# Second and third place change in seven products: the order of weight sums in a down projection

## The chip, the cores and the metric

The kernel runs on one core of one Trainium2 chip. The metric is the device time of one execution in microseconds (us). The engines of the core are named as in the profile: PE multiplies matrices, DVE (VectorE) and ACT (ScalarE) work element by element, POOL (GpSimd) does a few small operations and issues some transfers, and SP issues most of the transfers. The transfers themselves run on 16 DMA engines.

## What is computed

Two layers, each of three residual blocks with a layer norm behind it. The change lies in the first and the third block of each layer, the feed-forward ones, so it is passed four times in an execution.

```python
def swiglu_ffn(x, w_gu, w_down):
    a, u = jnp.split(x @ w_gu, 2, axis=-1)
    return (jax.nn.silu(a) * u) @ w_down
...
for l in range(DEPTH):
    x = layer_norm(DEEPNORM_ALPHA * x + 0.5 * swiglu_ffn(x, ffn1_w_gu[l], ffn1_w_down[l]), ln1_g[l], ln1_b[l])
    x = layer_norm(DEEPNORM_ALPHA * x + hybrid_mixer(...), ln2_g[l], ln2_b[l])
    x = layer_norm(DEEPNORM_ALPHA * x + 0.5 * swiglu_ffn(x, ffn2_w_gu[l], ffn2_w_down[l]), ln3_g[l], ln3_b[l])
```

Here x has 512 tokens of 1024 features, and the inner width DFF is 2816, that is 22 chunks of 128. Everything is in float32.

## The kernel before

**Numbers in two parts.** Every operand of a matmul is split in a rounded part and a rest (`split`, L158): ACT writes the rounded part (L159, tiles with an h at the end: `uh` for weights, `hh` for inner activations), and DVE then writes the rest (L160, tiles with an l: `ul`, `hl`). `mm3` (L165) makes three matmuls of such a pair: rounded by rounded (L168), and the two mixed ones (L169, L170 in the trace).

**Weights in units.** Weights come as a list of items that is taken in a fixed order. A unit is 128 x 1024 numbers and lies in one of six buffers (`UBUFS`). `Weights.pump` (L50) makes the next unit, that is its split and, where needed, the load of its raw weights, as soon as one of the six is given back by `W.done`; raw weights lie in two buffers of 1 MB (`raw`). `W.get` hands out units in the order of the list. So the place at which a split is asked for is set by the place in the list and by the `W.done` that frees a buffer.

**The gate stage** (`glu7`, L517) makes the inner activations `hT` two chunks at a time, in seven products of its own with `xh`, `xl`, `Th`, `Tl`. In its last pass (fp = 10) it ends with two groups on `Th`, `Tl`, an activation (L556) and a product on DVE (L563). Two kinds of its instructions matter below: the sums that DVE reads out of a bank before PE writes it again (L547), and L556 and L563, after which the memory pool of the gate stage is closed (L624) and the pool of the down stage, with `hh`, `hl` and `s1`, is opened in the same memory.

**The down stage** multiplies the first eight chunks of `hT` by the first 1024 rows of the down weights in seven products instead of eight (Strassen's scheme in Winograd's form). The activations are cut in A11, A12, A21, A22 (first figure: tokens 0 to 255 or 256 to 511; second: chunks 0 to 3 or 4 to 7), the weights in B11, B12, B21, B22 (rows, columns). Each product has two halves g = 0, 1 of two chunks, each half takes one unit, and one half is 12 matmuls of 512 columns. The order before:

| product | banks | activations | weights |
|---|---|---|---|
| 1 | low | A11 | B11 |
| 2 | left | A12 | B21 |
| 3 | high | `fifth`: A21 - A22 | B11 + B12 |
| 4 | low, on top | what `fifth` left in A11 | B11 + B12 + B22 |
| 5 | right | `third`: A12 plus that | B22 |
| 6 | low, on top | what `fifth` left in A21 | B12 + B22 |
| 7 | low, on top | A22 | B12 + B22 + B11 + B21 |

Between them, `into` (L710) adds finished banks into the residual `Y` with the instruction L714, two for each pair of banks; chunk 8 comes ahead of product 7, and chunks 9 to 21 behind it, as plain products.

**The sums of weights** are made by the DMA engines (`down_items`, L340). For each half g a tile `R[g]` has two columns. When the first unit of B11 is made, `begin` (L351) lets SP load B11 and B12 into them (L356), and lets POOL issue accumulating transfers (`add`, L348, its instruction L349) of 512 KB each: B12 onto column 0 of both halves, then B22 onto column 1 of both. `cut` (L363) makes a unit from a column (the splits `uh<-R` and `ul<-R`), and where it says so it then issues the next `add` onto the same column: B22 after the first cut of column 0, B21 after the second. The adds are kept in the order in which the program states them; `R` uses the two buffers (tag "S") in which the gate stage held its own weight sums.

**The operands** come from a generator, `operands` (L663), two halves ahead of their use: `ahead` (L696) starts with the two halves of A11, split early, and the first operand of the list, and each half of a product asks for one more before its matmuls (L724). `fifth` (L642) makes three subtractions on DVE (L647 into `s1`, L648 and L649 in place in A21 and A11) and then splits `s1`. `operand` splits a part of `hT` as it is. There are four pairs of `hh` and `hl`.

**Order.** After the very first pass `self.pin` is False: the splits aren't held to the order of the program. When the program is built, a scheduler lays out a fixed order for each engine from dependencies, the order of the program as priority and its own estimates of durations. On the chip each engine then takes its instructions in that order; one that waits holds up all behind it.

Of the kernel before, what the change touches and what calls it, by code (L numbers as in the profile page):

```python
# [24 lines left out]
ALPHA = (2 * DEPTH) ** 0.25  # L25
# [67 lines left out]
class Trunk:  # L93
# [246 lines left out]
    def down_items(self, w, key, R, row):  # L340

        def block(i, j, g):
            r0 = i * 512 + g * 256
            return w[r0 : r0 + 256, j * 512 : (j + 1) * 512].rearrange("(k p) c -> p k c", p=P)

        def add(g, x, i, j):  # L348
            self.tc.keep_in_program_order(self.nc.gpsimd.dma_start(R[g][:, x], block(i, j, g), accum_op=ALU.add))  # L349

        def begin(go):  # L351
            def f(v, hi, lo):
                for g in range(2):
                    R[g] = self.spool.tile([P, 2, 2, 512], F32, tag="S", name=self.nm("R"), bufs=2)
                    for x in range(2):
                        self.nc.sync.dma_start(R[g][:, x], block(0, x, g))  # L356
                    add(g, 0, 0, 1)
                for g in range(2):
                    add(g, 1, 1, 1)
                return go(v, hi, lo)  # L360
            return f

        def cut(g, x, *after):  # L363
            def go(v, hi, lo):
                hv, lv = (t.rearrange("p (k c) -> p k c", k=2) for t in (hi, lo))
                self.split(hv, lv, R[g][:, x])
                for a in after:
                    add(g, *a)
                return hv, lv
            return (None, None, None, go)  # L370

        p1, p2, p3 = (self.wide_item(w, j * 512, i, (key, "b", i, j)) for i, j in ((0, 0), (1, 0), (1, 1)))
        p1[0] = p1[0][:3] + (begin(p1[0][3]),)
        return (p1 + p2 + [cut(g, 0, (0, 1, 1)) for g in range(2)]
                + [cut(g, 0, (0, 1, 0)) for g in range(2)] + p3 + [cut(g, 1) for g in range(2)]
                + [row] + [cut(g, 0) for g in range(2)])

# [97 lines left out]
    def ffn(self, g_, b, out=None):  # L475
        nc, tc, W = self.nc, self.tc, self.W
        with ExitStack() as ctx:
# [150 lines left out]
            def pair():  # L628
                return [pool.tile([P, 512], F32R, tag=tag, name=self.nm(tag), bufs=TAIL) for tag in ("hh", "hl")]

            def part(g, i, j):

                return hT[:, j * 4 + 2 * g : j * 4 + 2 * g + 2, i * 256 : (i + 1) * 256]

            def operand(src):
                hh, hl = (v.rearrange("p (f t) -> p f t", f=2) for v in pair())
                self.split(hh, hl, src)
                return hh, hl
# [3 lines left out]
            def fifth(g):  # L642

                a11, a21, a22 = part(g, 0, 0), part(g, 1, 0), part(g, 1, 1)
                hh, hl = (v.rearrange("p (f t) -> p f t", f=2) for v in pair())
                s1 = self.s1[:, g]
                nc.vector.tensor_sub(s1, a21, a22)  # L647
                nc.vector.tensor_sub(a21, a11, a21)  # L648
                nc.vector.tensor_sub(a11, s1, a11)  # L649
                self.split(hh, hl, s1)  # L650
                return hh, hl

            def third(g):

                nc.vector.tensor_add(part(g, 0, 1), part(g, 0, 1), part(g, 0, 0))
                return operand(part(g, 0, 1))

            def whole(f):
                hh, hl = pair()
                self.split(hh, hl, hT[:, f, :])  # L660
                return hh, hl

            def operands():  # L663
                for g in range(2):
                    yield operand(part(g, 0, 1))
                for g in range(2):
                    yield fifth(g)
                for g in range(2):
                    yield operand(part(g, 0, 0))
                for g in range(2):  # L670
                    yield third(g)
                for g in range(2):
                    yield operand(part(g, 1, 0))
                yield whole(8)
                for g in range(2):
                    yield operand(part(g, 1, 1))
                for f in range(9, NF):
                    yield whole(f)

            def seventh(banks, u, h, new):  # L680

                for f in range(2):
                    for i, b_ in enumerate(banks):
                        ts = slice(i * P, (i + 1) * P)
                        self.mm3(b_, (h[0][:, f, ts], h[1][:, f, ts]), (u[0][:, f, :], u[1][:, f, :]),
                                 new and f == 0, False, skip_group_check=True)
                self.step()

            def down(f, u, h, t, q):
# [3 lines left out]
                         skip_group_check=True)  # L693

            split = operands()
            ahead = [(hv[0][:, g], hv[1][:, g]) for g in range(2)] + [next(split)]  # L696

            def chunk(f):
                u, h = W.get(), ahead.pop(0)
                ahead.append(next(split))  # L700
                for i, (t, q) in enumerate(((0, 0), (0, 1), (1, 0), (1, 1), (2, 1), (3, 1), (2, 0), (3, 0))):
                    down(f, u, h, t, q)
                    if i % 4 == 3:
                        self.step()
                W.done()

            low, high = [acc[t][0] for t in (2, 3)], [acc[t][1] for t in (2, 3)]
            left, right = [acc[t][0] for t in (0, 1)], [acc[t][1] for t in (0, 1)]

            def into(banks, t0, q, scale, sign=ALU.add):  # L710

                for i, b_ in enumerate(banks):
                    y = self.Y[:, t0 + i, q * 512 : (q + 1) * 512]
                    nc.vector.scalar_tensor_tensor(out=y, in0=y, scalar=scale, in1=b_, op0=ALU.mult, op1=sign)  # L714

            for n, (banks, new, more) in enumerate((
                    (low, True, (0, 0, ALPHA)), (left, True, None), (high, True, (0, 1, ALPHA)),
                    (low, False, (0, 1, 1.0, ALU.subtract)), (right, True, None),
                    (low, False, (2, 1, ALPHA, ALU.subtract)), (low, False, None))):
                if n == 6:  # L720
                    chunk(8)
                for g in range(2):
                    u, h = W.get(), ahead.pop(0)
                    ahead.append(next(split))  # L724
                    seventh(banks, u, h, new and g == 0)
                    W.done(2 if n == 0 and g == 1 else 1)
                if more:
                    into(banks, *more)
# [400 lines left out]
```

## Time and profile before

| what | value |
|---|---|
| runs before, median (lowest to highest of 3) | 1840.15 us (1836.89 to 1842.22) |
| the profiled execution, its own time | 1839.6 us |
| span of that execution in the profile | 1837.8 us |
| mean granted clock of PE | 0.991 |
| moved by DMA | 205.87 MB, 112 GB/s on the mean |
| accumulating adds, POOL | 32 of 512 KB, 8.1 us from issue to landing (median) |
| loads into `R`, SP | 16 of 512 KB, 5.2 us |
| first matmul of the four down stages | 233.58, 795.17, 1143.14, 1705.70 us from the span's start |

How to read it: the profile shows one execution. "Busy" is the time in which an engine had an instruction under way; matmuls overlap, so PE can be busy and yet not at its full pace. In a row of a timeline stand the start, the duration, the engine, the line, the operation, what it writes and reads, and in brackets how long the engine had been idle before and what ended that. In a table of waits stand the total, the number and the longest. The granted clock is the share of its full clock that PE was allowed. In the table of stretches (length, busy time and instructions of each engine, clock, share of the DMA engines' time, GB/s) the DMA share can come out a little over 1.

### The profile page before, as it was taken

The numbers are of one execution on the slowest core, as the hardware profiler recorded it, in microseconds if no ns is written. First come the engines' busy times: TensorE is split into PE (matmuls) and PEld (weight loads), VectorE is DVE, ScalarE is ACT, GpSimd is POOL, SyncE is SP. The second block draws the span as 40 slices with busy tenths as digits, with TensorE's granted clock in tenths as the row PEclk, the third lists the DMA queues.
The fourth block names the chain that finished last, engine by engine and source line by source line (L and its number), as shares of the span: only waits on it lengthen the run. The fifth ranks groups of instructions, "written<-read, shape, count | busy, mean of one in ns | idle before, by whom it ended". The sixth has DMA issues, their size and how long they took to land.

```text
span 1837.8 us, 29295 instructions
## 1 busy us (share of the span) xinstructions
PE 1801.7 (98%) x12074; PEld 1634.5 (89%) x12074; DVE 1341.4 (73%) x1942; ACT 880.5 (48%) x1439; POOL 123.8 (7%) x104
## 2 busy tenths in 40 slices
PE   9999989999999999989999999899999999999898
PEld 9999978887789999978899999788877899999786
DVE  7888785656758788876688887747567687887745
ACT  4455553278713455554235555432785234555530
POOL 0000010111110000020000001001111100000101
PEclk9999999999999999999999999999999999999999
DMA  5233475223122323484223236641233122334731
GB/s 183 93 127 103 148 196 161 64 81 91 49 91 69 116 93 101 140 195 161 92 65 97 93 101 196 163 155 47 81 93 92 46 93 93 112 118 137 185 114 46
DMA packets 151991, 205.87 MB, mean 112 GB/s; under 512 B 4657, under 2 KB 116017, under 8 KB 151857
## 3 DMA queue, kind: packets, MB, share of 16 engines
q1 hardware_dynamic: 143152, 187.23, 31.5%
q0 software_dynamic: 8704, 16.78, 5.3%
q8 instruction: 94, 1.54, 0.4%
q14 instruction: 41, 0.33, 0.1%
HBM read 201.89 MB, written 2.10 MB: 111 GB/s over the span
## 4 chain that ended last, share of the span: by engine, by line
PE 81%; DVE 5%; issue 5%; ACT 4%; DMA 3%; POOL 1%; SPq 0%; POOLq 0%; DVEq 0%; ACTq 0%
PE ps L170 26%; PE ps L168 26%; PE ps L169 26%; DMA R<-in_ffn_w_down_dram 2%; ACT sw L898 1%; PE ps L428 1%; DVE ul L160 1%; DMA raw<-in_ffn_w_gu_dram 1%; ACT uh L159 1%; ACT b L940 1%; ACT b L934 1%; DVE Y L464 1%; POOL sw L900 1%; DVE st L454 1%; DVE Y L461 0%
## 5 line engine op out<-in xcount | busy, mean ns | idle before, releaser
L168 PE MATMUL ps<-xh,uh 128*128 128x256 f32 (+1 forms) x1616 | 482.0, 298 | 0.2 <-ACT uh L159 0.2
L170 PE MATMUL ps<-xh,ul 128*128 128x256 f32 (+1 forms) x1616 | 479.1, 297 | 0.7 <-DVE ul L160 0.7
L169 PE MATMUL ps<-xl,uh 128*128 128x256 f32 (+1 forms) x1616 | 478.7, 296 | 0.4 <-DVE xl L160 0.2
L159 ACT CAST uh<-raw 128x1024 fp32r<-128x1024 f32 (+1 forms) x325 | 291.7, 914 | 220.2 <-PE ps L169 137.4
L160 DVE TENSOR_TENSOR ul<-raw,uh 128x1024 fp32r<-128x1024 f32 (+1 forms) x325 | 336.9, 1050 | 81.7 <-ACT uh L159 81.0
L168 PE MATMUL ps<-Th,uh 128*128 128x256 f32 x1152 | 319.1, 277 | 0.0
L169 PE MATMUL ps<-Tl,uh 128*128 128x256 f32 x1152 | 318.7, 277 | 0.0
L170 PE MATMUL ps<-Th,ul 128*128 128x256 f32 x1152 | 318.3, 276 | 0.0
L168 PEld LDWEIGHTS ps<-xh,uh 128*128 128x128 f32 x1616 | 307.9, 191 | 10.6 <-issue 1.6
L170 PEld LDWEIGHTS ps<-xh,ul 128*128 128x128 f32 x1616 | 307.9, 191 | 9.6 <-DVE ul L160 1.1
L169 PEld LDWEIGHTS ps<-xl,uh 128*128 128x128 f32 x1616 | 308.0, 191 | 8.5 <-DVE xl L160 0.8
L168 PE MATMUL ps<-uh,hh 128*128 128x512 f32 x640 | 256.2, 400 | 16.0 <-ACT hh L159 16.0
L170 PE MATMUL ps<-uh,hl 128*128 128x512 f32 x640 | 254.6, 398 | 4.8 <-DVE hl L160 4.8
L169 PE MATMUL ps<-ul,hh 128*128 128x512 f32 x640 | 252.4, 394 | 0.0
L159 ACT CAST uh<-S 128x1024 fp32r<-128x1024 f32 x144 | 151.1, 1049 | 153.0 <-PE ps L169 148.0
L160 DVE TENSOR_TENSOR ul<-S,uh 128x1024 fp32r<-128x1024 f32 x144 | 175.9, 1222 | 62.3 <-ACT uh L159 61.7
L168 PEld LDWEIGHTS ps<-Th,uh 128*128 128x128 f32 x1152 | 216.7, 188 | 0.0
L169 PEld LDWEIGHTS ps<-Tl,uh 128*128 128x128 f32 x1152 | 216.7, 188 | 0.0
L170 PEld LDWEIGHTS ps<-Th,ul 128*128 128x128 f32 x1152 | 216.3, 188 | 0.0
L168 PEld LDWEIGHTS ps<-uh,hh 128*128 128x128 f32 x640 | 122.7, 192 | 42.3 <-ACT hh L159 17.7
L170 PEld LDWEIGHTS ps<-uh,hl 128*128 128x128 f32 x640 | 122.2, 191 | 35.3 <-DVE hl L160 7.4
L169 PEld LDWEIGHTS ps<-ul,hh 128*128 128x128 f32 x640 | 122.4, 191 | 26.8
(141 smaller groups left out, 2249.2 us busy)
## 6 DMA issues: line engine op xcount, KB each, us to landing
raw<-in_ffn_w_gu_dram SPq DMA_DIRECT2D x86, 1024.0 KB, 5.6
raw<-in_ffn_w_down_dram SPq DMA_DIRECT2D x40, 1024.0 KB, 5.0
raw<-in_w_in_dram SPq DMA_DIRECT2D x18, 1024.0 KB, 5.3
R<-in_ffn_w_down_dram POOLq DMA_DIRECT2D x32, 512.0 KB, 8.1
R<-in_ffn_w_down_dram SPq DMA_DIRECT2D x16, 512.0 KB, 5.2
raw<-in_w_in_dram SPq DMA_DIRECT2D x8, 512.0 KB, 4.6
raw<-in_w_out_dram SPq DMA_DIRECT2D x8, 512.0 KB, 6.1
raw<-in_w_out_dram SPq DMA_DIRECT2D x4, 1024.0 KB, 4.9
```

Source lines behind the costliest of these rows:

```text
L159: a = self.nc.scalar.copy(hi, src)
L160: b = self.nc.vector.tensor_sub(lo, src, hi.bitcast(F32))
L168: mm(out, ah, bh, start=start, stop=False, **kw)
L169: mm(out, ah, bl, start=False, stop=False, **kw)
L170: mm(out, al, bh, start=False, stop=stop, **kw)
L428: nc.tensor.transpose(b[:, c * P : (c + 1) * P], src[:, c * P : (c + 1) * P], self.ident)
L454: nc.vector.bn_stats(out=st[:, h, :], in_=y[:, hs])
L464: nc.vector.scalar_tensor_tensor(out=y[:, hs], in0=y[:, hs], scalar=rs, in1=b[:, hs], op0=ALU.mult, op1=ALU.add)
L898: nc.scalar.copy(sw[q * 32 : q * 32 + 32, :n], src[o * 32 : o * 32 + 32, :n])
L900: nc.gpsimd.tensor_mul(sw[:, :n], sw[:, :n], S)
L934: nc.scalar.activation(s[kv][:, cc, :nk], s[kv][:, cc, :nk], AF.Exp, bias=m[:, cc : cc + 1], scale=SCALE, accum_out=den[:, cc : cc + 1])
L940: nc.scalar.activation(s[kv][:, cc, :nk], s[kv][:, cc, :nk], AF.Copy, scale=den[:, cc : cc + 1])
```

## The change

The third product of the table above becomes the second, and the second the third. In the list of weights the two units of B11 + B12 come ahead of those of B21; in `operands` `fifth` comes ahead of the split of A12; and the triple of banks, flag and `into` moves with them, so that the high banks are added into `Y` one product earlier. Nothing else is changed, and the number of instructions of every kind stays.

```diff
-        return (p1 + p2 + [cut(g, 0, (0, 1, 1)) for g in range(2)]
+        return (p1 + [cut(g, 0, (0, 1, 1)) for g in range(2)] + p2
                 + [cut(g, 0, (0, 1, 0)) for g in range(2)] + p3 + [cut(g, 1) for g in range(2)]
                 + [row] + [cut(g, 0) for g in range(2)])
...
             def operands():
                 for g in range(2):
+                    yield fifth(g)
+                for g in range(2):
                     yield operand(part(g, 0, 1))
-                for g in range(2):
-                    yield fifth(g)
                 for g in range(2):
                     yield operand(part(g, 0, 0))
...
-                    (low, True, (0, 0, ALPHA)), (left, True, None), (high, True, (0, 1, ALPHA)),
+                    (low, True, (0, 0, ALPHA)), (high, True, (0, 1, ALPHA)), (left, True, None),
                     (low, False, (0, 1, 1.0, ALU.subtract)), (right, True, None),
                     (low, False, (2, 1, ALPHA, ALU.subtract)), (low, False, None))):
```

## The prediction, made before the changed kernel ran

> **What bounds the kernel now.** The page comes first, then the list of waits, then the four places that the waits point at. TensorE (PE) is busy for nearly the whole span, so only what it waits for can be won or lost. The kernel has four down projections of seven products each, and among the waits of PE two rows belong to them alone (columns: total us, times, longest):
>
> ```profile
> PE 1801.7 (98%) x12074; PEld 1634.5 (89%) x12074; DVE 1341.4 (73%) x1942; ACT 880.5 (48%) x1439; POOL 123.8 (7%) x104
> ```
>
> ```profile
> PE ps L168 <- ACT hh L159: 16.0, 4, 4.3
> ```
>
> ```profile
> PE ps L170 <- DVE hl L160: 4.8, 4, 1.6
> ```
>
> So once per down projection PE waits for the rounded operand `hh`, and right after for its rest `hl`: 20.8 us together. The table of stretches prices it. Its first row is the second product of the first down projection, undisturbed; the other four are the third product of each (columns: length, PE busy, granted clock, DMA share, GB/s):
>
> ```profile
> 239.05:244.53 5.48, 4.97 (x17) 1.00 1.10 262
> 244.53:257.31 12.78, 6.45 (x16) 0.73 0.81 136
> 806.12:819.69 13.57, 6.87 (x16) 0.75 0.81 135
> 1154.10:1167.96 13.86, 6.87 (x16) 0.75 0.81 140
> 1716.66:1730.26 13.60, 6.38 (x16) 0.78 0.81 135
> ```
>
> The four third products take 53.8 us where 4 x 5.48 = 21.9 would do: **31.9 us** are lost, 8.0 per stage. 20.8 are waits; the other 11.1, 2.8 per stage, are matmuls at half clock after the wait. Two stretches around the first wait and one around a shorter wait elsewhere show when the clock falls (PE, PEld, DVE, ACT, POOL busy, clock):
>
> ```profile
> 246.34:249.75 3.41, 1.09 (x5) 0.56 (x3) 1.68 (x2) 1.28 (x2) 0.09 (x1) 1.00 0.68 124
> 249.75:256.58 6.83, 4.30 (x9) 2.98 (x10) 6.83 (x10) 5.90 (x8) 2.34 (x2) 0.50 0.76 116
> ```
>
> ```profile
> 453.00:456.41 3.41, 2.32 (x36) 2.09 (x32) 2.42 (x4) 3.34 (x7) 0.00 (x0) 1.00 0.33 91
> ```
>
> 3.41 us with PE 68% idle were followed by 6.83 us at half clock; 3.41 us with 32% idle were not.
>
> Why is the operand late? ACT's and VectorE's (DVE) rows in order of time, first stage:
>
> ```profile
> 228.12 1.05 ACT L159 CAST uh<-raw 128x1024 fp32r<-128x1024 f32 x1 [1.46 <-PE ps L169]
> 229.07 0.84 ACT L553 ACTIVATE Q<-Q 128x768 f32<-128x768 f32 x1
> 230.97 1.05 ACT L159 CAST uh<-raw 128x1024 fp32r<-128x1024 f32 x1 [1.06 <-PE ps L169]
> 232.42 0.38 ACT L556 ACTIVATE s<-ps 128x256 f32<-128x256 f32 x1 [0.39 <-PE ps L170]
> 233.66 1.05 ACT L159 CAST uh<-R 128x1024 fp32r<-128x1024 f32 x1 [0.86 <-PE ps L169]
> 234.62 1.14 ACT L159 CAST hh<-hT 128x512 fp32r<-128x512 f32 x2
> 235.66 0.62 ACT L159 CAST hh<-s 128x512 fp32r<-128x512 f32 x1
> 236.70 1.05 ACT L159 CAST uh<-R 128x1024 fp32r<-128x1024 f32 x1 [0.42 <-DMA R<-in_ffn_w_down_dram]
> 247.00 1.05 ACT L159 CAST uh<-R 128x1024 fp32r<-128x1024 f32 x1 [9.24 <-DMA R<-in_ffn_w_down_dram]
> 249.51 1.05 ACT L159 CAST uh<-R 128x1024 fp32r<-128x1024 f32 x1 [1.47 <-DMA R<-in_ffn_w_down_dram]
> 250.53 0.62 ACT L159 CAST hh<-s 128x512 fp32r<-128x512 f32 x1
> ```
>
> ```profile
> 230.35 0.42 DVE L547 TENSOR_TENSOR Q<-Q,ps 128x256 f32<-128x256 f32 x1
> ...
> 233.85 0.42 DVE L563 SCALAR_TENSOR_TENSOR hT<-ps,s 128x256 f32<-128x256 f32 x1 [0.36 <-PE ps L170]
> 234.31 0.69 DVE L647 TENSOR_TENSOR s<-hT 128x512 f32<-128x512 f32 x1
> 234.92 1.22 DVE L160 TENSOR_TENSOR ul<-R,uh 128x1024 fp32r<-128x1024 f32 x1
> 236.05 1.29 DVE L160 TENSOR_TENSOR hl<-hT,hh 128x512 fp32r<-128x512 f32 x2
> ...
> 248.07 1.23 DVE L160 TENSOR_TENSOR ul<-R,uh 128x1024 fp32r<-128x1024 f32 x1 [7.19 <-ACT uh L159]
> ```
>
> Call X0, X1 the sums B11+B12 of the two halves g, and Y0, Y1 the same with B22 added. 233.66 and 236.70 split X0 and X1; 247.00 and 249.51 split Y0 and Y1, which only the fourth product needs. 250.53 is the operand of the **third** product, half 1. It stands behind Y0 and Y1 in both queues and waits for two transfers that it does not use. PE stood idle for it, not for a weight.
>
> What holds the sums is POOL's queue and the DMA engines:
>
> ```profile
> 221.72 1.35 POOL L349 DMA_DIRECT2D R<-in_ffn_w_down_dram  x1 [220.41 <-DMA R<-in_ffn_w_down_dram]
> 227.15 2.44 POOL L349 DMA_DIRECT2D R<-in_ffn_w_down_dram  x2 [4.08 <-DMA R<-in_ffn_w_down_dram]
> 231.15 1.23 POOL L349 DMA_DIRECT2D R<-in_ffn_w_down_dram  x1 [1.55 <-DMA R<-in_ffn_w_down_dram]
> 236.88 1.21 POOL L349 DMA_DIRECT2D R<-in_ffn_w_down_dram  x1 [4.51 <-DVE hl L160]
> 241.12 1.20 POOL L349 DMA_DIRECT2D R<-in_ffn_w_down_dram  x1 [3.02 <-DVE Y L714]
> ```
>
> ```profile
> L349 POOL DMA_DIRECT2D R<-in_ffn_w_down_dram x1: 1707/1707/1707, 227.9 to 227.9; - x1
> DMA to landing us min/median/max: 13.0/13.0/13.0
> ```
>
> ```profile
> L349 POOL DMA_DIRECT2D R<-in_ffn_w_down_dram x1: 1207/1207/1207, 791.5 to 791.5; - x1
> DMA to landing us min/median/max: 5.9/5.9/5.9
> ```
>
> ```profile
> 243.00:246.50 3.50, 0.00 (x0) 1.00 1.13 206
> ```
>
> The six issues are, in order, X0, X1, the two sums in R's column 1, Y0, Y1. X1, issued at 227.15, is there for the split at 236.70, some 9.5 us later. The third lands at 227.9 + 13.0 = 240.9, and only 0.2 later Y1 is issued, although X1's split had ended by 239.1 (236.70 + 1.05 + 1.22, with a little between): I read this as at most three sums under way at once. With all DMA to themselves the sums move at 206 GB/s, so one of 0.524 MB takes 2.55 us. In the second stage X1 lands at 791.5 + 5.9 = 797.4.
>
> **The change part by part.** No instruction and no transfer is added or removed; four pairs change places.
>
> *Unit order.* X0's split comes to where B21's first split stands (228.12), X1's to 230.97, B21's to 233.66 and, the sixth buffer being free only after half a product, some 3 us on. These places follow from unit buffers: each row there was released by PE, not by data. But X1 is not there at 230.97. Will the built order still put it there? The order of now placed Y0 and Y1 ahead of work whose inputs were there some 8 us before them, so whoever laid it out took the sums for much faster than they are; I take it that X1's split stands at its early place, ahead of the activation L556. Bounds: no wait at all (X1 set behind L556), or the full one.
>
> *What the full wait costs, first stage.* ACT stands at X1 until 236.70, as now. DVE takes X1's rest at 237.78 (1.08 after the cast starts, as 248.07 after 247.00) for 1.13 (234.92 to 236.05); then L563 at 238.9 instead of 233.85, and with it the memory in which the operands lie comes free: L647 at 239.4 (0.46 on). There follow 0.61 for L647 (234.31 to 234.92), 1.13 for B21's rest, 2 x 0.61 for L648 and L649 and 0.69 for the `hl` of half 0, now the operand of the **second** product: 243.0. X0 is late too: issued at 221.72, with 7.6 to 9.5 us to land, it comes 1.2 to 3.1 after its place; the middle moves DVE's L547 (230.35), on which the last group of the gate products waits, enough to hold PE 0.7 us. So the second product would begin at 239.75 and need `hl` 0.46 later, at 240.2; it waits 2.8. Loss: 0.7 + 2.8 = **3.5 us**. Half 1's operand is 1.13 us under PE's pace behind it and costs nothing.
>
> *The other stages.* In the second, the third product starts at 806.12, so the first at 795.16, and X1 lands 2.2 after it where the first stage has 3.1; X0 then is early enough. Loss 3.5 - 0.9 = 2.6. I take 3.0 for the other two, between these: **12.1 us** in all.
>
> *Operand order.* `fifth` of half 1 is now asked for before Y0 and Y1, so the wait of now is gone. Behind them stands half 1 of A12, needed 13.7 + 3.5 us after the first product's start; its cast needs only `hT` and has been ready for long, its `hl` may queue on DVE behind both Y splits and two L714.
>
> *The transfers that move.* SP's load of rows f = 8, 9 waits for B21's buffer; its second split moves from 230.97 to after the `fifth` pair, so 1 MB leaves the time in which the sums run. X1 lands at 236.6, then four sums at 2.55 each: Y0 at about 244.3 and Y1 at 246.8 instead of 249.5. Then A12's `hl` is ready at 246.8 + 0.06 + 1.08 + 1.13 + 1.2 + 0.69 = 251.0, and PE wants it at 233.58 + 17.7 = 251.2: just covered. If that cover is gone, see the third rival. The load itself is wanted two products later. `into` for the high banks moves one product forward: 2 L714, DVE's, off the path. PSUM banks: during the first product PE waits for nothing now, and that stays.
>
> *Clock.* The new wait is 2.8 us in 3.41 at most, 82% idle if a window falls right, above the 68% that halved the clock; with a bad fall it is under it. I take one and a half of the four stages at 2.8: **4.2 us**.
> The Trainium skill, page "TensorE: Matmul & The Clock Gate", section "Part 1: The HAM clock gate", has the clock fall after at least one idle window of about 3.4 us. By that rule the new waits, all shorter, cost nothing more and the sum would be 4 us lower; the stretch from 246.34, a third busy and yet followed by half clock, speaks against so strict a reading.
>
> *Sum.* 1839.6 (the profiled execution: span 1837.8 and 1.8 around it) - 31.9 + 12.1 + 4.2 = **1824**. The profiled run lies 0.6 under the median of the three, so the same figure stands for the median.
>
> **The rivals.**
> 1. *No new wait.* X1's split is laid behind L556, as now. For it: now it stands behind the three operand casts. Against: there a buffer held it, which is free 5.7 us earlier then. Loss 0.7: 1839.6 - 31.9 + 0.7 = 1808.
> The Trainium skill, page "DMA: Bandwidth & Descriptors", section "Anatomy of one DMA — SWDGE (gpsimd) path", fits such a transfer as 2.0 us + bytes at 436 GB/s, an estimate of 3.2 us here; X1 would then be there at 230.4, in time, and the result would be this rival's. The row of 9.5 us (here) and 5.9 us (second stage) disagrees, so it adds nothing to the chance.
> 2. *The wait only moves.* `fifth` of half 1 stays behind Y0 and Y1 on ACT: their buffers come free about 1 us after its input is ready, no wide margin. Then its cast follows Y1's, 246.8 + 1.1 + 0.6 = 248.5 where PE wanted 241.8: 6.7 lost, with half clock 8 to 9, as now: 1837 to 1843.
> 3. *Slower: Y1 late, with A12 behind it.* If Y1 lands at 249.5 as now, because the row load does not give way or the sixth sum waits longer, A12's `hl` comes at 253.7 against 251.2: 2.5 us, with one fall of the clock or two 3.5 + 2.5 + 2.8 = 8.8 or 11.6 against 8.0 per stage: 1843 to 1854. It turns slower than now from 1.7 us of wait with one fall, that is with Y1 at about 248.7, 1.9 later than I reckon.
>
> **How the numbers follow.** Forecast 0.52, between 1819 (no fall of the clock) and 1831 (four falls); rival 1 0.22; rival 2 0.14; rival 3 0.12. Three runs of this kernel spread over 5.3 us, 0.3%, so less can't be told from no change. The forecast and rival 1 lie over 0.3% below (under 1834.6): 0.74; rival 2 within: 0.14; rival 3 above: 0.12. The range goes from 1806, rival 1 with 2 us to spare, to 1839, half of rival 2, and leaves out some 0.19.
>
> **What would show it.** Right: no idle PE in what was the third product; two casts of R on ACT ahead of L556, the second ended by DMA at some 236.7; PE waiting 2 to 3 us for `hl` at the start of the second product; 0 to 2 stretches of clock 0.50 there. Wrong: X1's cast behind L556 (rival 1), a cast `hh<-s` behind two DMA-ended casts of R (rival 2), or PE idle at the third product, half 1, for `hl<-hT` (rival 3).

## The result and the profile after

| what | before | after |
|---|---|---|
| runs, median (lowest to highest) | 1841.08 us (1836.89 to 1842.22, 4 runs) | 1823.55 us (1822.39 to 1826.58, 4 runs) |
| ratio of the runs, with its 95% interval | | 0.9911 (0.9891 to 0.9932) |
| the profiled execution, its time and span | 1839.6, 1837.8 us | 1826.58, 1824.8 us |
| mean granted clock of PE | 0.991 | 0.995 |

The profiled execution after is the slowest of its four runs. In it the down stages start at 233.96, 792.39, 1134.76 and 1695.03 us.

To compare kernels I use one measure below: the **excess**. The first 168 matmuls of a down stage (six products and chunk 8) take 7 x 5.49 = 38.4 us at full pace; what they take beyond that, summed over the four stages, is 32.4 us before and 18.0 after. The rows for the first stage from the table of stretches, before and then after (length, busy PE, PEld, DVE, ACT, POOL, clock, DMA share, GB/s):

```profile
233.58:279.30 45.72, 40.88 (x171) 32.65 (x170) 34.80 (x45) 21.87 (x28) 4.84 (x4) 0.93 0.73 178
```

```profile
233.96:276.48 42.52, 40.57 (x171) 32.57 (x170) 35.88 (x47) 23.02 (x30) 4.84 (x4) 0.96 0.75 188
```

45.72 and 42.52 against 38.4. In all, 14.4 us are won there, and the spans differ by 13.0: 0.4 is lost ahead of the first stage, and 1.0 behind these matmuls of the third, where 24 matmuls go on taking 5.60 us instead of 5.49. Of PE's waits after, these three belong to the change:

```profile
PE ps L168 <- ACT hh L159: 4.7, 4, 1.9
PE ps L170 <- DVE hl L160: 4.0, 5, 0.9
...
PE ps L168 <- DVE Q L547: 0.7, 1, 0.7
```

The old pair of waits (16.0 and 4.8) is down to 4.7 and 4.0, and there is a new one of 0.7. But they are not the old waits made shorter. The second products of the four stages and one third product show where they are:

```profile
240.65:249.01 8.36, 7.48 (x25) 5.71 (x25) 8.36 (x12) 4.99 (x7) 0.63 (x2) 0.80 0.98 237
249.01:254.50 5.49, 5.49 (x25) 4.51 (x24) 5.49 (x9) 3.55 (x5) 1.86 (x2) 1.00 0.77 128
798.18:805.74 7.56, 6.20 (x24) 4.47 (x25) 7.44 (x11) 3.94 (x5) 0.00 (x0) 1.00 1.07 246
1141.86:1150.26 8.40, 7.51 (x24) 5.72 (x25) 7.73 (x12) 4.45 (x6) 0.54 (x1) 0.80 1.04 239
1702.59:1712.20 9.61, 8.73 (x24) 6.61 (x25) 9.61 (x14) 6.02 (x8) 1.76 (x2) 0.64 0.80 197
```

The third product runs at its full pace (5.49 where it took 12.8 to 13.9), and the second now takes 7.6 to 9.6. The stretch between the first matmul of a stage and the first of its second product is longer too: 240.65 - 233.96 = 6.69 in the first stage. Why is told by ACT's and DVE's rows in order of time, first stage:

```profile
229.78 1.05 ACT L159 CAST uh<-R 128x1024 fp32r<-128x1024 f32 x1 [3.76 <-DMA R<-in_ffn_w_down_dram]
...
236.50 1.05 ACT L159 CAST uh<-R 128x1024 fp32r<-128x1024 f32 x1 [4.93 <-DMA R<-in_ffn_w_down_dram]
237.45 0.37 ACT L556 ACTIVATE s<-ps 128x256 f32<-128x256 f32 x1
...
239.98 0.62 ACT L159 CAST hh<-s 128x512 fp32r<-128x512 f32 x1 [1.21 <-DVE s L647]
...
243.44 0.62 ACT L159 CAST hh<-s 128x512 fp32r<-128x512 f32 x1 [1.90 <-DVE s L647]
...
247.00 1.05 ACT L159 CAST uh<-R 128x1024 fp32r<-128x1024 f32 x1 [1.47 <-DMA R<-in_ffn_w_down_dram]
247.95 0.61 ACT L159 CAST hh<-hT 128x512 fp32r<-128x512 f32 x1
```

```profile
232.00 0.41 DVE L547 TENSOR_TENSOR Q<-Q,ps 128x256 f32<-128x256 f32 x1
...
238.72 0.42 DVE L563 SCALAR_TENSOR_TENSOR hT<-ps,s 128x256 f32<-128x256 f32 x1
239.18 0.69 DVE L647 TENSOR_TENSOR s<-hT 128x512 f32<-128x512 f32 x1
...
241.52 0.68 DVE L160 TENSOR_TENSOR hl<-s,hh 128x512 fp32r<-128x512 f32 x1
...
250.42 0.69 DVE L160 TENSOR_TENSOR hl<-hT,hh 128x512 fp32r<-128x512 f32 x1
```

229.78 and 236.50 are the splits of X0 and X1, each released by its transfer. X1 stands ahead of L556, and ACT is idle for 4.93 us in front of it, so L556, L563, L647 and the operand behind them are late: `hh` at 240.6, `hl` at 242.2. The two casts `hh<-s` are now both ahead of Y1's split (247.00), which is why the third product no longer waits. 250.42 is the rest of A12's second half.

POOL's rows show the last two sums issued ahead of the Y splits. SP's row is the load of the weight rows of chunks 8 and 9 (1 MB, called the row load below); the last fence is that load before:

```profile
236.66 1.21 POOL L349 DMA_DIRECT2D R<-in_ffn_w_down_dram  x1 [5.22 <-DMA R<-in_ffn_w_down_dram]
239.52 1.20 POOL L349 DMA_DIRECT2D R<-in_ffn_w_down_dram  x1 [1.65 <-DVE hT L563]
```

```profile
244.57 0.37 SPq L265 DMA_DIRECT2D raw<-in_ffn_w_down_dram  x1
```

```profile
233.51 0.37 SPq L265 DMA_DIRECT2D raw<-in_ffn_w_down_dram  x1
```

The load has moved from 0.1 us ahead of the first matmul of the stage to 10.6 behind it. Y1 landed 13.0 us after that matmul (12.3 to 14.1 over the four stages), where it had landed at 15.9 to 16.4.

And the clock. Stretches around the first matmuls of the second product, first and second stage:

```profile
239.20:242.61 3.41, 1.46 (x6) 0.60 (x5) 3.41 (x5) 1.57 (x2) 1.20 (x1) 1.00 1.13 205
242.61:246.02 3.41, 3.41 (x10) 2.67 (x9) 3.41 (x6) 2.09 (x3) 0.00 (x0) 0.51 0.97 170
...
797.00:800.40 3.40, 2.34 (x10) 1.31 (x9) 3.40 (x6) 1.57 (x2) 1.18 (x1) 1.00 1.13 205
800.40:803.80 3.40, 2.92 (x13) 2.09 (x12) 3.40 (x5) 2.09 (x3) 0.00 (x0) 1.00 1.10 206
```

PE idle for 57% of 3.41 us was followed by half clock, idle for 31% was not. The third stage has such a fall of 3.41 us too. The fourth has one of 6.83, and in its first half PE waited once more:

```profile
1703.55:1706.96 3.41, 2.76 (x7) 2.18 (x8) 3.41 (x5) 1.57 (x3) 0.00 (x0) 0.50 1.00 178
```

Before, all four stages had falls of 6.83.

### The profile page after: what moved, and what is told of

It reads as the page before. It is cut to its first block, busy times and chain, and to the rows that moved or that the text cites. A ratio compares the mean times of both kernels' runs of the same rounds, so it can differ in the third digit from the quotient of the medians.

```text
span 1824.8 us, 29291 instructions
## 1 busy us (share of the span) xinstructions
PE 1800.6 (99%) x12074; PEld 1632.9 (89%) x12074; DVE 1339.8 (73%) x1942; ACT 878.7 (48%) x1439; POOL 123.8 (7%) x104
## 4 chain that ended last, share of the span: by engine, by line
PE 82%; issue 7%; DVE 5%; ACT 3%; DMA 2%; POOL 1%; SPq 0%; POOLq 0%; DVEq 0%; ACTq 0%
PE ps L170 27%; PE ps L169 26%; PE ps L168 26%; DMA R<-in_ffn_w_down_dram 1%; ACT sw L898 1%; POOL sw L900 1%; PE ps L428 1%; DMA raw<-in_ffn_w_gu_dram 1%; DVE ul L160 1%; DVE Y L464 1%; ACT uh L159 1%; DVE st L454 1%; DVE Y L461 0%; PE ps L1008 0%; DVE Y L452 0%
## 5 line engine op out<-in xcount | busy, mean ns | idle before, releaser
L170 PEld LDWEIGHTS ps<-uh,hl 128*128 128x128 f32 x640 | 122.0, 191 | 31.9 <-DVE hl L160 6.4
```

Source lines behind the costliest of these rows:

```text
L170: mm(out, al, bh, start=False, stop=stop, **kw)
```

## The experiments

**The theory** after the result: the 32 us before were the place of half 1 of `fifth` behind Y0 and Y1 in the queues of ACT and DVE; what is left is X1's split ahead of L556; and Y1 lands sooner because the row load no longer runs beside the sums. **The rivals:** Y1 and Y0 are late by the sums' own rate, and the order of the queues matters little; or DVE simply has too much to do. Times are medians, the ratio is to before on the same chip, the excess is that of the profiled execution.

| run | edit | us | ratio (95%) | excess |
|---|---|---|---|---|
| 1 | before, `fifth` ahead of Y | 1826.35 | 0.9918 (0.9905 to 0.9931) | 19.1 |
| 2 | before, row load later in the program | 1841.01 | 0.9999 (0.9990 to 1.0008) | 32.4 |
| 3 | 1 and 2 together | 1825.06 | 0.9914 (0.9901 to 0.9928) | 17.9 |
| 4 | after, no sum for X1 | 1819.86 | 0.9884 (0.9867 to 0.9900) | 15.0 |
| 5 | after, X1's unit behind B21's | 1836.81 | 0.9979 (0.9970 to 0.9988) | 28.0 |
| 6 | before, row load held behind Y1's issue | 1836.38 | 0.9979 (0.9969 to 0.9989) | 28.6 |
| 7 | 1, with the load held so | 1824.22 | 0.9913 (0.9898 to 0.9928) | 16.3 |
| 8 | before, row load held behind Y0's split | 1826.61 | 0.9921 (0.9908 to 0.9935) | 18.9 |
| 9 | 5, with `fifth` and A12 ahead of Y, load held as in 6 | 1819.86 | 0.9891 (0.9874 to 0.9907) | 10.6 |
| 10 | 1, with `into` directly behind its product | 1816.87 | 0.9873 (0.9857 to 0.9889) | 8.4 |
| 11 | 9, with `into` so, load held as in 8 | 1811.51 | 0.9840 (0.9827 to 0.9853) | 5.6 |
| 12 | 10, load held as in 8 | 1808.95 | 0.9831 (0.9818 to 0.9844) | 1.2 |

The span less the excess is 1804 to 1807 us in every one of these profiles (before 1837.8 - 32.4 = 1805.4, after 1806.8, run 12 1806.2 - 1.2 = 1805.0): what the runs differ by lies in these products.

**Run 1: the queue alone, in the old order of products.**

```diff
-            ahead = [...] + [next(split)]
+            ahead = [...] + [next(split), next(split)]
...
-                    ahead.append(next(split))
                     seventh(banks, u, h, new and g == 0)
+                    ahead.append(next(split))
...
-                self.split(hh, hl, s1)
+                self.pin = True; self.split(hh, hl, s1); self.pin = False
...
-                self.split(hv, lv, R[g][:, x])
+                self.pin = after == ((0, 1, 0),); self.split(hv, lv, R[g][:, x]); self.pin = False
```

> The kernel before, with the products in their old order; only the operands are asked for one half sooner, and the splits of `fifth` are held ahead of the splits of Y0 and Y1 on ACT and DVE. The row load stays where it was. Queue theory (PE waited for an operand that stood behind splits which waited for Y0 and Y1): the wait in the third product goes, it takes 5.5 to 6.0 us instead of 13.5; what is late next is the operand of the fourth product, whose rest stands on DVE behind the split of Y1 (landing some 16 us after the first product, rest ready some 19), 2 to 2.5 us in the fourth product; 1812 to 1820 us. Arrival theory (what counts is when Y0 and Y1 arrive, in the changed kernel some 3 us sooner): they arrive as late as before, so PE loses about what it lost, only one product later: 1834 to 1842 us.

The third product took 5.49 us in every stage although Y1 landed at 15.7 to 16.9, as late as ever: the wait was the queue's, and the rival that puts it down to the arrival is out. The time missed its range by 6, because of a wait that was not foreseen. PE's waits there, and DVE's rows in the first stage:

```profile
PE ps L170 <- DVE hl L160: 8.3, 4, 2.6
PE ps L168 <- DVE Y L714: 5.3, 3, 1.8
```

```profile
261.97 1.21 DVE L160 TENSOR_TENSOR ul<-R,uh 128x1024 fp32r<-128x1024 f32 x1
263.11 1.27 DVE L714 SCALAR_TENSOR_TENSOR Y<-Y,ps 128x512 f32<-128x512 f32 x2
```

The `hl` is the expected wait of the fourth product for Y1. The other is new: the fourth product's last matmul had been issued by 256.16, but the L714 that empties its banks stands behind a row of splits until 263.11, and the sixth product, which writes those banks, starts at 263.93.

**Runs 2 and 3: the row load later in the program.** In the loop of `pump` that loads ahead, the row unit is passed over until B22's second split has been made (run 3: with the edits of run 1).

```diff
-                if held == 2:
+                if held == 2 or (r2 and r2[1:] == ("d", 4) and (r2[0], "b", 1, 1) in self.raws
+                                 and self.last[(r2[0], "b", 1, 1)] >= self.emitted):
                     break
```

> The kernel before, with nothing moved but SP's load of the rows f = 8, 9, which is issued only after the second split of B22. All orders on PE, ACT, DVE and POOL stay. Both theories: Y1 lands some 2.5 us sooner (13 to 13.5 us after the first product instead of 15.9 to 16.4). Arrival theory: that is most of the gain of the change, 1822 to 1828 us. Queue theory: the operand of the third product still stands behind Y1, so the wait of PE only shrinks, by 2 to 3 us a stage, and the clock still falls in most: 1826 to 1832 us, and PE still waits for `hh<-s` and `hl` in the third product.

> The two edits together on the kernel before (old order of products, `fifth` ahead of Y0 and Y1, row load after B22's split). Queue theory: with Y1 landing at 13 to 13.5 us the operand of the fourth product is ready by 16.5, just when PE wants it, so no wait over 0.6 us is left in the seven products and the clock stays full: 1807 to 1812 us, below the changed kernel by 11 to 16. Arrival theory: no better than the row load alone, 1822 to 1828 us.

Both say nothing of the load: SP still issued it 0.07 us ahead of the first matmul in every stage, since nothing but its buffer held it there. A later place in the program is no later start. Run 3 is a repeat of run 1.

**Run 4: the changed kernel without X1's sum.**

```diff
-                    add(g, 0, 0, 1)
+                    (g or add(g, 0, 0, 1))
```

> The changed kernel without the first accumulating transfer of half 1 (B12 onto column 0 of R[1]), so one weight sum lacks a term and five sums run instead of six before Y1. X1's split then needs only SP's load. Theory that the rest of the loss is X1's transfer at the head of ACT's queue: ACT no longer waits there, the second product begins at once and takes 5.5 to 6.2 us in all stages, no half clock: 1807 to 1813 us. Rival that DVE's six instructions of `fifth` are what the second product waits for: the wait stays at 2 us or more a stage, 1820 to 1824 us.

The second product took 5.49 in all four stages, so X1's transfer was its whole wait, and the rival is out. But the time missed its range by 7, since part of the gain was lost again at another place. PE's waits:

```profile
PE ps L170 <- DVE hl L160: 5.4, 3, 1.8
PE ps L168 <- ACT hh L159: 3.1, 3, 1.3
```

They lie in the third product (9.8, 10.8, 10.6 and 5.8 us), half 1: A12's operand behind the Y splits, the place of the third rival. The products start sooner, and the cover of A12 is used up.

**Run 5: X1 later.** X0's unit stays in front, X1's goes behind B21's two, and `get` hands it out in its turn.

```diff
-        return (p1 + [cut(g, 0, (0, 1, 1)) for g in range(2)] + p2
+        return (p1 + [cut(0, 0, (0, 1, 1))] + p2 + [cut(1, 0, (0, 1, 1))]
...
-    def get(self):
+    def get(self, n=0):
...
-        return self.ready.pop(0)
+        return self.ready.pop(n)
...
-                    u, h = W.get(), ahead.pop(0)
+                    u, h = W.get(2 if n == 1 and g else 0), ahead.pop(0)
```

> The changed kernel, but the unit of X1 is made after the two units of B21 and not before them. So ACT takes X1's cast behind L556 and behind the cast of half 0 of `fifth`, and the second product should lose its wait (5.49 us instead of 7.6 to 9.6). What the first theory adds: B21's buffer is then free early again, the row load starts some 3 us after the first matmul instead of 10, Y1 lands late (14.5 to 16) and A12's `hl` of half 1, which stands behind Y1's rest on DVE, holds the third product for some 4 us with half clock behind it (the place of the third rival): 1833 to 1841, that is, no better than before although the wait of the second product is gone. Rival, the wait of the second product is all there is to win: 1808 to 1812.

As the theory had it. No wait in the second product; the row load 2.6 to 2.9 after the first matmul and Y1 at 15.6 to 15.9; PE's waits, and DVE's rows of the first stage:

```profile
PE ps L170 <- DVE hl L160: 12.3, 4, 3.1
PE ps L168 <- ACT hh L159: 4.1, 4, 1.2
```

```profile
249.85 1.23 DVE L160 TENSOR_TENSOR ul<-R,uh 128x1024 fp32r<-128x1024 f32 x1
251.00 0.69 DVE L160 TENSOR_TENSOR hl<-hT,hh 128x512 fp32r<-128x512 f32 x1
```

A12's rest comes right behind Y1's, 18 us after the first matmul. So X1's early place, which costs the second product its wait, is also what holds back B21's second split and with it the row load: the wait at X1 buys an earlier Y1. Taking the wait away alone leaves a gain of 3 to 4 us out of some 17.

**Runs 6, 7 and 8: a row load that really is later.** POOL clears one column of the row's buffer, pinned behind an issue of `add`; SP's load must wait for that. The condition in `pump` sets behind which one (runs 6 and 7: Y1's issue, n = 3; run 8: the next one, behind Y0's split, n = 4).

```diff
+            r = self.raw()
+            if key[1:] == ("d", 4):
+                self.tc.keep_in_program_order(self.nc.gpsimd.memset(r[:, :1], 0.0))
...
-                if held == 2:
+                if held == 2 or (r2 and r2[1:] == ("d", 4) and self.emitted < self.last[(r2[0], "b", 1, 0)] + n):
                     break
```

> The order of before in everything, but the row load (rows f = 8, 9) is made to wait, in earnest this time: one column of its buffer is cleared by POOL behind the issue of Y1, and the load waits for that, so that its 1 MB should start some 8 us after the first matmul of a stage and not at -0.07. Theory that the load takes its bandwidth from the sums (step S of the prediction: 1 MB leaves the time in which the sums run): Y1 lands some 2.5 us sooner, at 13.0 to 13.8 after the first matmul instead of 15.9 to 16.8; the third product still waits for the operand behind it, but 1.5 to 2.5 us less per stage, perhaps with fewer falls of the clock: 1822 to 1833. Rival, sums are held by their own rate or by the three under way: Y1 lands where it does now, 1838 to 1842.

> The order of before, with the operands sooner and `fifth` ahead of the Y splits (the pinned kernel, 1826), and the row load made to wait as in the first of these runs. Y1 landing some 2.5 us sooner takes away the wait of the fourth product (1.6 to 2.6 us per stage) and, if it came from DVE running behind after that wait, also the 1.77 at L714 ahead of the sixth product: 1808 to 1814. If the second wait has its own cause (L714 standing behind the splits on DVE whatever Y1 does): 1816 to 1820.

> The order of before, with the row load made to wait until the issue behind Y0's split, some 12 us after the first matmul (it ran from 7.3 to 16 beside Y1 in the run before this). Theory that the row load takes its time from the sums that run beside it: Y0 at 10.5 to 11, as there, and now Y1 at 12.5 to 13.3 instead of 15 to 16; the operand behind it then holds the third product for only 0.5 to 1 us at `hh` and 1 to 1.5 at `hl`: 1815 to 1825. Rival, Y1 is held by its own issue or by the number of sums under way: it lands at 15 or later, 1834 to 1840.

Third stage of run 6, POOL's clearing of the column, SP's load and ACT's splits of Y0 and Y1, and then the splits in run 8:

```profile
1146.82 0.59 POOL L260 MEMSET raw<- 128x1 f32 x1
```

```profile
1147.43 0.37 SPq L268 DMA_DIRECT2D raw<-in_ffn_w_down_dram  x1
```

```profile
1150.54 1.05 ACT L159 CAST uh<-R 128x1024 fp32r<-128x1024 f32 x1 [6.38 <-DMA R<-in_ffn_w_down_dram]
1155.54 1.04 ACT L159 CAST uh<-R 128x1024 fp32r<-128x1024 f32 x1 [3.96 <-DMA R<-in_ffn_w_down_dram]
```

```profile
1149.09 1.05 ACT L159 CAST uh<-R 128x1024 fp32r<-128x1024 f32 x1 [6.24 <-DMA R<-in_ffn_w_down_dram]
1151.67 1.05 ACT L159 CAST uh<-R 128x1024 fp32r<-128x1024 f32 x1 [1.53 <-DMA R<-in_ffn_w_down_dram]
```

The stage starts at 1140.18 in run 6 and at 1138.86 in run 8. In run 6 Y0 landed at 10.3, where it had landed at 13.8 before, but then the load began 1.3 us behind Y1's issue, and Y1 came at 15.3. The time, 1836.38, lies between the two ranges and decides nothing, since the load had only moved from one sum to the next. In run 8, with the load out of the way of both, Y1 came at 12.7 in this stage and at 13.1 to 14.5 in the others. So the load takes its time from the sums beside it, about 2.6 us of Y1 (mean 13.5 against 16.1), and that alone is worth 15 us in the old order of products. 1826.61 is just above its range: Y0 and Y1 came up to 1.2 later than I had reckoned in two stages, and three falls of the clock were left. Run 7 missed both its ranges: Y1 still came at 15.2 to 16.0, as in run 6, and the fifth product still took 7.7 to 7.8.

**Runs 9, 10, 11 and 12: all of it together, in both orders of products.** Run 9 takes run 5, pins the operands of `fifth` and A12 as in run 1 and holds the load as in run 6. Runs 10, 11 and 12 also move `into`:

```diff
                     seventh(banks, u, h, new and g == 0)
+                    if more and g:
+                        into(banks, *more)
                     ahead.append(next(split))
                     W.done(2 if n == 0 and g == 1 else 1)
-                if more:
-                    into(banks, *more)
```

> The last kernel plus two things: the operands are asked for one half sooner and those of `fifth` and A12 are kept in the order of the program ahead of the Y splits, and the row load waits for the issue of Y1 by the cleared column. If the three waits found so far (X1 in front of L556, operands behind Y, Y1 late because of the row load) are all that the seven products lose: no wait at the second and third product, Y1 landing at 12.5 to 14 and the fourth product (second half at 19.2 after the first matmul) not waiting either: loss under 2 us per stage in all, 1808 to 1815. Rival, DVE's own work has become the bound there (as the wait for L714 ahead of the sixth product in the pinned kernel suggests): 1.8 us per stage at the fifth or sixth product, 1815 to 1822.

> The order of before, operands sooner and pinned (1826.35), with `into` directly behind the second half of its product in the program. If the wait ahead of the sixth product (fifth product 7.76 us in three stages, 6.19 in one) comes from L714's place behind a split, it goes and the wait of the fourth product for Y1 (1.6 to 2.6 us) stays: 1817 to 1821. If DVE is late because Y1 held it, the fifth product stays at 7 us or more: 1824 to 1828.

> The kernel with X1 late, pinned operands and the late row load (1819.86), with two changes. First, `into` stands in the program directly behind the second half of its product, ahead of the next operand and of the unit that the freed buffer allows; theory: the 1.2 us for which PE waited at L714 ahead of the sixth product (7.5 us for the fifth product in all four stages instead of 5.5) come only from L714 standing behind that unit's split in DVE's order, so they go: 8 us. Second, the row load waits for the issue behind Y0's split, so that it starts at about 12 after the first matmul and not at 8.5, beside Y1; where it ran beside Y1, Y1 landed at 15.7 in the second stage and the fourth product took 7.6: that goes too, 2 us. Together 1808 to 1813. Rival, DVE simply has too much to do there, and the wait comes back at another place: 1816 to 1821.

> The order of products of before, with everything that the runs have found: operands sooner and `fifth` pinned ahead of the Y splits, `into` directly behind its product, and the row load behind the issue that follows Y0's split. If the waits come from the queues and the arrival of Y1 alone, the order of the products is worth nothing by itself: Y1 lands at 12.7 to 14.5 after the first matmul, A11's operand of half 0, now behind Y1's rest, is ready at 15.5 to 17.5 against a need at 16.5, and the loss of the seven products falls to 1 to 5 us: 1808 to 1813, level with the best kernel of the changed order (1811.5). Rival, the changed order has an advantage of its own: 1814 to 1818, with the wait of the fourth product left.

Run 9 came out at its rival's time, by 1.2 us of wait at the same L714 in each stage and a fifth product of 7.1 to 7.5. Run 10 shows that its cause isn't the amount of DVE's work but the place of L714. The fifth product of its first stage, and the L714 of the low banks, which now comes 4.6 us behind the fourth product and not 7.0 (263.11 - 256.16 in run 1):

```profile
256.43:261.92 5.49, 5.49 (x26) 4.44 (x24) 5.49 (x8) 4.11 (x7) 0.00 (x0) 1.00 0.46 184
```

```profile
261.01 1.27 DVE L714 SCALAR_TENSOR_TENSOR Y<-Y,ps 128x512 f32<-128x512 f32 x2
```

Run 10 came out 0.1 us below its range, runs 11 and 12 in theirs. What was left in run 10 is A11's operand behind Y1, 0.3 to 1.3 us of `hh` and 0.6 of `hl` at the start of each fourth product. Run 11 had 1.8 us of `hl` and 0.7 of `hh` left in the four stages together. Run 12 has the old order of products and none of these waits at all; what is left of its excess is a slower pace, 5.6 to 5.9 us, in the fifth and sixth products of three stages. Its first two stages, where the first took 45.72 before and 42.52 after:

```profile
233.29:271.71 38.42, 38.42 (x171) 31.56 (x169) 34.80 (x45) 21.63 (x29) 4.96 (x5) 1.00 0.82 199
787.59:826.47 38.88, 38.88 (x170) 31.32 (x169) 34.79 (x45) 21.41 (x29) 4.92 (x5) 1.00 0.79 195
```

It lies some 15 us under the changed kernel (ratios 0.9831 and 0.9911), with the products where they were. The intervals of runs 11 and 12 overlap, so the new order of products isn't shown to be worth anything by itself: it was one way to get `fifth` out from behind Y0 and Y1, and it paid for that with X1. Not tried: run 12's edits on the changed kernel with X1 in its early place.

## Why the prediction was right

**The old wait goes.** All 31.9 us of it: the third product takes 5.49 to 5.62. Runs 1 and 8 confirm both halves of the reading, the queue and the late transfer in front of it.

**X1 ahead of L556.** The step that was chosen between two bounds came out as chosen: cast at 236.50 (236.70 forecast), L563 at 238.72 (238.9), L647 at 239.18 (239.4). `hl` was done at 242.2 against 243.0, since L649 went behind it. So the waits of the second product were smaller than reckoned: 1.07 + 0.88 = 1.95 in the first stage and 8.7 in all four, where the forecast has 11.4. Half 1, put at nothing, waited 0.48 in the second stage.

**X0 late.** Forecast 0.7 at L547, measured 0.7, and only in the first stage, as argued.

**The clock, mis-sized.** This is the step that was wrong: "one and a half of the four stages at 2.8". The clock fell in three. Of the 18.0 us of excess 8.7 are waits. In the first two products the rest is 2.1 us in the first and third stage (falls of 3.41 us) and 3.4 in the fourth (6.83): 7.6 where the sum has 4.2. Another 1.7 came without a fall, and the sum has no term for it. The second stage lost 0.9; some 0.5 of that belongs to its three waits, for the profile counts a gap from the end of a matmul of 0.39 us, while at full pace the next one starts after 0.23. The other 0.8 is a slower pace behind the second product, mostly in the third stage (5.60 per product at a granted clock of 1.00), whose cause stays open. Together this makes 9.3 against 4.2. It was too little by 5.1, the waits too much by 2.7, so the sum 16.3 (with the 0.7) should have been 18.0 + 0.7 = 18.7. The profiled execution, 1826.58, shows that difference: 2.6 above the forecast. That the median, 1823.55, lies 0.5 from the forecast is luck: the other three executions had a mean clock of 0.996 to 0.998 against 0.995, which fits fewer or shorter falls, but no trace of them was kept.
The Trainium skill, page "TensorE: Matmul & The Clock Gate", section "Part 1: The HAM clock gate", has the clock fall after an idle window; by that reading none of these falls should have been there. The stretch from 239.20, idle for 57% of it, disagrees. The same section calls the windows free-running, and that the trace does bear out. The falls of one execution start whole multiples of 3.413 us apart: before, at 249.75, 812.95, 1161.11 and 1724.31, which is 165, 102 and 165 of them. In run 8 the third product waited 2.1 us in the third stage and kept its clock, and 2.3 in the fourth and lost it. The first two rows are these products; the other two are the stretch of that grid with the most idle time in each, idle for 46% and for 62%:

```profile
1149.81:1158.00 8.19, 6.06 (x26) 4.35 (x24) 7.83 (x11) 6.09 (x9) 2.54 (x3) 1.00 0.63 122
1706.77:1716.65 9.88, 7.62 (x25) 5.52 (x24) 9.39 (x13) 6.52 (x9) 2.51 (x3) 0.83 0.70 160
1153.44:1156.85 3.41, 1.85 (x7) 1.20 (x8) 3.41 (x5) 2.85 (x5) 1.22 (x1) 1.00 1.01 155
1709.82:1713.23 3.41, 1.29 (x4) 0.79 (x5) 3.41 (x6) 3.11 (x5) 1.58 (x3) 1.00 0.74 113
```

**The row load and Y1.** Forecast 244.3 and 246.8 for Y0 and Y1, measured 244.4 and 246.9. Run 8 shows the cause: the load alone moves Y1 by 2.6 us. "At most three under way" fits as well: X0's split was over by 232.1, but POOL issued Y0 at 236.66, 0.26 us after X1 had landed. What sets the three isn't shown.

**The cover of A12.** Its rest was done at 250.42 + 0.69 = 251.1, as forecast (251.0); PE, later than reckoned, wanted it at 252.2.

**The rivals.** The first (no new wait) needed X1 behind L556; run 5 put it there, and the third rival's wait came with it, so 1808 wasn't to be had by that alone. The second (the wait only moves) fell with the casts at 239.98 and 243.44. The third did not happen here but is real: runs 4 and 5 show its wait, and in run 5, with Y1 at 15.7, it cost most of the gain.

## What to carry to other kernels

An operand that waits on an in-order queue behind work it doesn't use is worth more attention than the order of the work that uses it: here asking for it sooner, and emitting what frees a bank directly behind the product, did more than moving a product. When a load or a split moves, follow what it releases on other queues before removing its wait, for that wait may be what keeps a transfer out of another's way. And to delay a load, give it something to wait for; moving it in the program alone did nothing.

## What the runs showed of the hardware that was not expected

Half clock came after 3.41 us in which PE was idle for only 57%, it lasted 3.41 us in some cases and 6.83 in others, and waits of 2.1 and 2.3 us differed by a whole fall. Laid on the grid of 3.413 us that the falls of each execution mark, the profiles of before, after and the twelve runs agree (the last 50 us of each execution left aside). In the 3.41 us ahead of each of the 27 falls PE was idle for 51% or more, and no stretch idle for more than 52% kept its clock. A fall lasted 3.41 us where PE was idle for at most 10% of its first 3.41 us, and 6.83 where it was idle for 19% or more. So the place of a wait on the grid decides whether it costs a fall, and a second wait soon behind it doubles the fall. Three accumulating sums of 512 KB with all DMA to themselves landed some 2.5 us apart (7.55, 10.10 and 12.70 us after the first matmul in the third stage of run 12), while one that had a plain load of 1 MB beside it took 4 to 5 us after the sum before it (10.28 and 15.29 in the third stage of run 6).
